# Weight-block sums moved to VectorE and cut into three steps, PSUM pairs evacuated whole, convolution and gelu emitted later in a decoder layer on one Trainium2 core

## The chip, the cores and the metric

The kernel runs on one core of one Trainium2 chip. The metric is device time in microseconds: the median of three runs of the unchanged kernel, beside one execution that the hardware profiler recorded. PE is TensorE, DVE is VectorE, ACT is ScalarE, POOL is GpSimd, and SPq is the queue on SyncE that issues nearly all DMAs.

## What is computed

One inference step of a decoder layer, for 1024 prompt tokens and 8 x 4 sample tokens (T = 1056 columns), model width 1024, feed-forward width 4096, all in fp32:

```
h = rmsnorm(x);  q,k,v,gates = h @ w_in
mix = (sigmoid(gate_a)*(attention_a @ w_branch_a) + sigmoid(gate_b)*(attention_b @ w_branch_b)) @ w_out
x = x + rmsnorm(mix)
a, g = split(rmsnorm(x) @ w_up)              # 1024 -> 4096 and 4096
c = conv_b + sum_j conv_w[j] * shifted(a)    # causal depthwise, width 3
x = x + rmsnorm((gelu(c) * g) @ w_down)      # 4096 -> 1024
```

The change lies in the last stage of the mixer (`@ w_out` and its norm) and in the feed-forward part.

## The kernel before

**fp32 as three products.** Each operand is cut into a high part (fp32r, a cast on ACT) and a low part (operand minus high part). A product is three matmuls, high x high, low x high and high x low, summed in PSUM.

**Strassen over blocks.** `@ w_up` is done as 2 x 2 block products with seven products in place of eight (`PRODUCTS`, L1266). The weights' output side is walked in 32 steps `m`: `m = 2 fp` is the a half (convolution side) of feature block pair `fp`, `m = 2 fp + 1` the g half. In each, product `p` runs 0 to 6 over the blocks A11, A12, S2, S3, A22, S1, S4 of the raw weights, where S1 = A21 + A22, S2 = S1 - A11, S3 = A11 - A21, S4 = A12 - S2. One product is 24 matmuls of 128 x 128 by 264 columns: two column halves `c`, each with its own PSUM bank, four k blocks, three matmuls each. This document calls the seven products of the a half and the seven of the g half of one `fp` a pair of steps: 14 products.

**Order of the products.** `QUEUE` (L1268) is written out by hand: for the first six `m` (`EARLY`) first the products 0 and 1 of each (12 products, while the last norm of the mixer is still being made), then products 2 to 6 of each (30 products), and then seven for each further `m` (182). The engines' instruction streams are in the order of emission; each engine works through its own stream in order.

**What is done ahead.** At the start of product `i`, `up_cut` (L1291) prepares product `i + 4`: the block sums S1, S2, S3, S4 on POOL (L1301 to L1306), then in `cut_block` the cast to the high part on ACT (L1276) and the low part on POOL (L1277). Six `whl` tiles hold the two parts. Raw weights come by DMA into four `raw` tiles, asked for seven products ahead.

**What is done behind.** `evac` (L1351) takes each bank of 264 columns as soon as its 12 matmuls are done: product 0 by an ACT copy (L1357), the others by a DVE addition to a running sum. On the a side the sums land in `at` and `fr` (L1375). After products 5 and 6 of the a side `conv` (L1315) emits the convolution and the gelu of a feature block at once: two ACT instructions (L1320, L1321), four on DVE (L1323, L1324), the gelu on ACT (L1325), two copies on POOL. On the g side DVE multiplies the finished sums into `cv` (L1384). After the last product `u_sums` makes four differences on DVE (L1429 to L1432), which a `store` on SPq sends to DRAM at product 3 of the next step.

**Around it.** The `@ w_out` stage (loop at L1654) runs four column quarters of 264; its norms are made by `post` (L1162), whose steps are hung on the `hook()` calls between the products that follow. For the last quarter these products are the first of `QUEUE`. `spread` (L139) makes a norm: sums of squares by matmuls into a bank `ss`, the root on ACT and DVE, and a matmul into a bank `rb` that spreads the factor. `@ w_down` follows (loop at L1732): seven products of 16 units, `down` (L1547), with 24 matmuls per unit; `down_sum` (DVE), `down_high` (ACT) and `down_low` (weights' low part on POOL L1522, activations' low part on DVE L1523) run 4, 3 and 2 units ahead. `last_weights` (L1525) prepares the weights of the seventh product during the fifth and sixth, cast on ACT and low part on POOL. All PSUM tiles come from one pool of eight banks, `bank()`.

Of the kernel before, what the change touches and what calls it, by code (L numbers as in the profile page):

```python
# [48 lines left out]
def trunk(ctx, tc, a):  # L49
# [10 lines left out]
    psum = ctx.enter_context(tc.tile_pool(name="psum", bufs=8, space=PSUM))  # L60
# [78 lines left out]
    def spread(sums, w=CH, new=None):  # L139
# [3 lines left out]
        ss = bank("ss")  # L143
# [9 lines left out]
        rb = bank("rb")[:, 0:w]  # L153
# [950 lines left out]
    c_stack.close()  # L1104
    xpool = ctx.enter_context(tc.tile_pool(name="xpool", bufs=1, side="right", reuse_waits="tile"))
# [56 lines left out]
    def post(q, sums):  # L1162
# [108 lines left out]
    LA = 4  # L1271
# [8 lines left out]
    uraw, usum, uhl = {}, {}, {}  # L1280
# [34 lines left out]
    def conv(f):  # L1315
        at, fr, cv = fs[f]
# [20 lines left out]
    def put_a(f, q, emit):  # L1337

        at, fr = fs[f][0:2]
        n = CQ if q < NQ - 1 else CQ - NS  # L1340
        emit(at[:, 2 + q * CQ:2 + q * CQ + n], slice(0, n))
        if n < CQ:
            emit(fr[:, :, 2:6], slice(n, CQ))

    def seen(cols, t):
        t = t[:, cols]
        return t.rearrange("p (b s) -> p b s", s=4) if cols.stop - cols.start == NS else t

    scratch = []

    def evac(m, p, c, ps):  # L1351
        fp, part = divmod(m, 2)
        f = 2 * fp
        cs = slice(c * CQ, (c + 1) * CQ)
        s, t = u1[m], u2.get(m)
        if p == 0:
            act.copy(s[:, cs], ps)  # L1357
            return
        if p == 2:
            dve.tensor_tensor(s[:, cs], ps, s[:, cs], op=OP.add)  # L1360
            if m in ug1:
                cv = fs[f][2]
                dve.tensor_tensor(cv[:, cs], ug1[m][:, cs], cv[:, cs], op=OP.mult)
            return
        if p == 3:
            dve.tensor_tensor(t[:, cs], ps, s[:, cs], op=OP.add)
            return
        if p == 5:
            dve.tensor_tensor(s[:, cs], ps, s[:, cs], op=OP.add)

        fo = f + (p in (4, 5))
        base = t if p in (4, 5) else s
        q = c + 2 * (p in (5, 6))
        if part == 0:
# [531 lines left out]
```

## Time and profile before

| | us |
|---|---|
| median of 3 runs | 1925.26 |
| lowest and highest | 1924.42, 1927.51 |
| profiled execution, device time | 1927.82 |
| profiled execution, span of the core | 1925.8 |
| PE busy in the span | 1851.3 (96%) |
| DVE, ACT, POOL busy | 1206.2 (63%), 728.3 (38%), 1009.5 (52%) |
| mean granted TensorE clock, share of full speed | 0.986 |

The time of a run is the span plus about two microseconds around it. Matmuls are pipelined: a row gives a start, a time until the last modelled end, a count, and in square brackets the idle time before it with the instruction that ended it. Rows of one stream overlap by the depth of the pipeline, so the pace of PE is read from one start to the next.

### The profile page before, as it was taken

The numbers are of one execution on the slowest core, as the hardware profiler recorded it, in microseconds if no ns is written. First come the engines' busy times: TensorE is split into PE (matmuls) and PEld (weight loads), VectorE is DVE, ScalarE is ACT, GpSimd is POOL, SyncE is SP. The second block draws the span as 40 slices with busy tenths as digits, with TensorE's granted clock in tenths as the row PEclk, the third lists the DMA queues.
The fourth block names the chain that finished last, engine by engine and source line by source line (L and its number), as shares of the span: only waits on it lengthen the run. The fifth ranks groups of instructions, "written<-read, shape, count | busy, mean of one in ns | idle before, by whom it ended". The sixth has DMA issues, their size and how long they took to land.

```text
span 1925.8 us, 35025 instructions
## 1 busy us (share of the span) xinstructions
PE 1851.3 (96%) x13714; PEld 1764.4 (92%) x13714; DVE 1206.2 (63%) x2367; ACT 728.3 (38%) x1673; POOL 1009.5 (52%) x819
## 2 busy tenths in 40 slices
PE   8999999999999999989889999999999999999897
PEld 7977788888999999988879999999999999999897
DVE  8354427877720114659677666667776668778885
ACT  4366554434221115443323333333233334443541
POOL 3200015434422321355777888778878856555863
PEclk9999999999999999998999999999999999999998
DMA  7111225434622225762332332222323256635343
GB/s 250 55 62 68 80 70 178 146 111 130 201 94 95 80 98 176 268 217 74 137 122 95 112 100 85 84 84 95 106 90 111 79 184 223 208 123 187 112 134 130
DMA packets 102100, 243.35 MB, mean 126 GB/s; under 512 B 20416, under 2 KB 40960, under 8 KB 99200
## 3 DMA queue, kind: packets, MB, share of 16 engines
q1 hardware_dynamic: 100272, 240.63, 37.3%
q8 instruction: 108, 1.77, 0.4%
q10 hardware_dynamic: 1664, 0.49, 0.1%
q14 instruction: 56, 0.46, 0.1%
HBM read 197.83 MB, written 88.11 MB: 148 GB/s over the span
## 4 chain that ended last, share of the span: by engine, by line
PE 66%; POOL 16%; DVE 7%; issue 7%; ACT 3%; DMA 1%; SPq 0%; POOLq 0%; DVEq 0%; ACTq 0%
PE dense L232 32%; PE dense L1566 13%; PE dense L1410 12%; POOL whl L1277 8%; PE S L414 2%; PE O L486 2%; PE PT L474 2%; ACT whl L1276 2%; POOL raw L1306 1%; POOL S L1302 1%; POOL S L1301 1%; POOL raw L1304 1%; POOL ncv L1326 1%; DVE cv L1323 1%; DVE uc L1523 1%
## 5 line engine op out<-in xcount | busy, mean ns | idle before, releaser
L1410 PE MATMUL dense<-T,whl 128*128 128x264 f32 x3072 | 395.7, 288 | 28.0 <-POOL whl L1277 14.6
L1410 PEld LDWEIGHTS dense<-T,whl 128*128 128x128 f32 x3072 | 383.9, 191 | 36.9 <-POOL whl L1277 19.7
L232 PE MATMUL dense<-hh,wh 128*128 128x352 f32 x960 | 322.9, 339 | 0.7 <-ACT wh L97 0.2
L232 PE MATMUL dense<-hl,wh 128*128 128x352 f32 x960 | 310.6, 327 | 2.3 <-DVE hl L189 2.2
L232 PE MATMUL dense<-hh,wl 128*128 128x352 f32 x960 | 308.1, 324 | 0.6 <-DVE wl L98 0.6
L98 POOL TENSOR_TENSOR wl<-raw,wh 128x1024 fp32r<-128x1024 f32 (+1 forms) x46 | 106.4, 2314 | 378.0 <-ACT wh L97 375.7
L1410 PE MATMUL dense<-B,whl 128*128 128x264 f32 x2304 | 289.4, 285 | 9.5 <-ACT whl L1276 6.7
L1566 PE MATMUL dense<-uc,whl 128*128 128x264 f32 x2328 | 289.1, 286 | 8.0 <-DVE uc L1523 5.8
L1566 PEld LDWEIGHTS dense<-uc,whl 128*128 128x128 f32 x2328 | 286.3, 189 | 10.1 <-DVE uc L1523 7.1
L1410 PEld LDWEIGHTS dense<-B,whl 128*128 128x128 f32 x2304 | 284.7, 190 | 10.8 <-ACT whl L1276 7.3
L1277 POOL TENSOR_TENSOR whl<-raw,whl 128x512 fp32r<-128x512 f32 x160 | 221.1, 1400 | 121.7 <-ACT whl L1276 121.6
L232 PEld LDWEIGHTS dense<-hh,wh 128*128 128x128 f32 x960 | 181.6, 190 | 21.3 <-issue 14.0
L232 PEld LDWEIGHTS dense<-hl,wh 128*128 128x128 f32 x960 | 180.8, 189 | 3.2 <-DVE hl L189 3.2
L232 PEld LDWEIGHTS dense<-hh,wl 128*128 128x128 f32 x960 | 181.4, 190 | 1.2 <-DVE wl L98 1.2
L1276 ACT CAST whl<-raw 128x512 fp32r<-128x512 f32 x160 | 91.4, 615 | 171.4 <-POOL raw L1306 111.0
L1522 POOL TENSOR_TENSOR whl<-wr,whl 128x512 fp32r<-128x512 f32 x64 | 100.5, 1586 | 72.9 <-ACT whl L1509 72.9
L1323 DVE SCALAR_TENSOR_TENSOR cv<-a,cw,cv 128x1024 f32<-128x1024 f32 x64 | 82.1, 1282 | 89.8 <-ACT cv L1320 89.8
L1523 DVE TENSOR_TENSOR uc<-ur,uc 128x528 fp32r<-128x528 f32 x96 | 115.7, 1218 | 8.8 <-ACT uc L1507 8.7
L1277 POOL TENSOR_TENSOR whl<-S,whl 128x512 fp32r<-128x512 f32 x64 | 88.9, 1389 | 37.9 <-ACT whl L1276 37.9
L1276 ACT CAST whl<-S 128x512 fp32r<-128x512 f32 x64 | 39.9, 624 | 175.8 <-POOL S L1302 175.8
L1384 DVE TENSOR_TENSOR cv<-scratch,cv 128x264 f32<-128x264 f32 x116 | 100.1, 863 | 4.0
L1125 POOL TENSOR_TENSOR sq<-sq 128x264 f32<-128x264 f32 x39 | 34.8, 893 | 112.7 <-ACT sq L1665 91.0
(309 smaller groups left out, 3188.6 us busy)
## 6 DMA issues: line engine op xcount, KB each, us to landing
raw<-in_w_up SPq DMA_DIRECT2D x70, 512.0 KB
out_s<-in_cache SPq DMA_DIRECT2D x32, 1022.0 KB
ur<-ud SPq DMA_DIRECT2D x112, 264.0 KB
raw<-in_w_in SPq DMA_DIRECT2D x40, 512.0 KB
ud<-ts SPq DMA_DIRECT2D x16, 1056.0 KB
kv<-in_kv_s SPq DMA_DIRECT2D x64, 256.0 KB
wr<-in_w_down SPq DMA_DIRECT2D x48, 256.0 KB
ud<-cv SPq DMA_DIRECT2D x16, 528.0 KB
```

The costliest lines, as they stand in the source:

```text
L98: (eng or pool).tensor_tensor(l, raw, as32(h), op=OP.subtract)
L232: pe.matmul(ps, lhsT=w, rhs=x, start=(i == 0), stop=(i == len(mm) - 1))
L414: pe.matmul(S[h][:, 0:nk], lhsT=q[r, i * 128:(i + 1) * 128], rhs=k[r, blocks[i][0] * 128:blocks[i][0] * 128 + nk], start=True, stop=True)
L474: pe.transpose(PT[:, o:o + 128], s["P"][:, h, j * 128:(j + 1) * 128], ident)
L1276: act.copy(t[:, 0], src)
L1277: pool.tensor_tensor(t[:, 1], src, as32(t[:, 0]), op=OP.subtract)
L1323: dve.scalar_tensor_tensor(o, at[:, x:x + SEQ], w[x], o, op0=OP.mult, op1=OP.add)
L1384: dve.tensor_tensor(cv[:, qs], o, cv[:, qs], op=OP.mult)
L1410: pe.matmul(ps, lhsT=l, rhs=r, start=(k == 0 and n == 0), stop=(k == 3 and n == 2))
L1522: pool.tensor_tensor(dw[i][:, 1], dsrc.pop(i), as32(dw[i][:, 0]), op=OP.subtract)
L1523: dve.tensor_tensor(dx[i][:, 1], x[:, fp % 2], as32(dx[i][:, 0]), op=OP.subtract)
L1566: pe.matmul(dbanks[j, c], lhsT=l, rhs=r, start=(x == 0 and n == 0), stop=(x == FP - 1 and n == 2))
```

## The change

- **Three steps in place of one.** `up_cut` and `cut_block` are split. At the start of product `i`, `up_low(i + 3)` emits the low part on POOL, then `up_sum(i + 5)` the block sums, now on DVE, then `up_high(i + 4)` the cast on ACT. Before all of these stood at `i + 4`, with the sums on POOL.
- **PSUM in pairs of banks.** From the `@ w_out` stage on, PSUM is a ring of four tiles of two banks (`bank2`). The two column halves of a product share one tile, and one instruction of 528 columns evacuates both after the second half. `spread` takes `ss` and `rb` from the two banks of one tile. `down` and `down_evac` do likewise.
- **Convolution later.** `conv` becomes `conv_1` (all but the gelu) and `conv_2` (the gelu). For the block finished by product 5, `conv_1` comes after product 6; its gelu, and the other block's `conv_1`, one product later; the other gelu one more. The four differences of `u_sums` are handed out one per column half over the next two products (`spare`).
- **Smaller moves.** In the last quarter of `@ w_out` the residual additions of `post` are all on DVE, one addition of squares fewer is on POOL, raw weights of the first products are asked for from the first `ct` on, and no cache copy is issued there. In `@ w_down` the weights of the seventh product are all prepared in the sixth, low part on DVE; the sums of the fourth product's result (`down_sums`) are 12 instructions of 528 columns in place of 24 of 264, and one of them per unit in place of two.

```diff
@@
+    def bank2(name):
+        return pairs_of_banks[0].tile([128, 2, 512], F32, name=name, tag="pair", bufs=4)
...
-        ss = bank("ss")
+        if pairs_of_banks:
+            two = bank2("ss")
+            ss, rb = two[:, 0], two[:, 1]
...
-            (dve if ct % 2 else pool).tensor_tensor(m, m, x3[q][ct // 4][:, ct % 4], op=OP.add)
+            (dve if ct % 2 or last else pool).tensor_tensor(m, m, x3[q][ct // 4][:, ct % 4], op=OP.add)
...
-                if ct in (1, 2, 3, 5):
+                if ct in (1, 3, 5):
...
-    def cut_block(src):
-
-        t = wpool.tile([128, 2, 512], F32R, name="whl", tag="W", bufs=6)
-        act.copy(t[:, 0], src)
-        pool.tensor_tensor(t[:, 1], src, as32(t[:, 0]), op=OP.subtract)
-        return t
...
-            pool.tensor_tensor(s1, a21, a22, op=OP.add)
-            pool.tensor_tensor(s2, s1, a11, op=OP.subtract)
+            dve.tensor_tensor(s1, a21, a22, op=OP.add)
+            dve.tensor_tensor(s2, s1, a11, op=OP.subtract)
         elif p == 3:
-            pool.tensor_tensor(a21, a11, a21, op=OP.subtract)
+            dve.tensor_tensor(a21, a11, a21, op=OP.subtract)
         elif p == 6:
-            pool.tensor_tensor(a12, a12, usum[m][1], op=OP.subtract)
+            dve.tensor_tensor(a12, a12, usum[m][1], op=OP.subtract)
...
+    def up_high(i):
+        if i < len(QUEUE):
+            uhl[i] = wpool.tile([128, 2, 512], F32R, name="whl", tag="W", bufs=6)
+            act.copy(uhl[i][:, 0], usrc[i])
+
+    def up_low(i):
+        if i < len(QUEUE):
+            pool.tensor_tensor(uhl[i][:, 1], usrc.pop(i), as32(uhl[i][:, 0]), op=OP.subtract)
+
+    def up_ahead(i):
+
+        up_loads(i + 7)
+        up_low(i + 3)
+        up_sum(i + 5)
+        up_high(i + 4)
...
+        ps = bank2("dense")
         for c in range(2):
-            ps = bank("dense")[:, 0:CQ]
...
-            evac(m, p, c, ps)
+            if c:
+                evac(m, p, ps)
             hook()
-        if part == 0 and p in (5, 6):
-            fo = f + (p == 5)
-            fs[fo].append(T_("cv"))
-            conv(fo)
+            if spare:
+                spare.popleft()()
+        if after:
+            after.popleft()()
+        if part == 0 and p == 6:
+            conv_1(f + 1)
+            after.append(lambda: (conv_2(f + 1), conv_1(f)))
+            after.append(lambda: conv_2(f))
...
-        pool.tensor_tensor(wk[fp][:, 1], x, as32(wk[fp][:, 0]), op=OP.subtract)
+        dve.tensor_tensor(wk[fp][:, 1], x, as32(wk[fp][:, 0]), op=OP.subtract)
...
-        if p == 4 and fp >= 4:
-            last_weights(fp - 4)
-        elif p == 5 and fp < 4:
-            last_weights(FP - 4 + fp)
+        if p == 5:
+            last_weights(fp)
...
-            if q == NQ - 1 and ct > 3:
-                up_loads(2 * (ct - 4))
+            if q == NQ - 1:
+                up_loads(min(2 * ct, 6))
...
-        if i + LA < len(QUEUE):
-            up_cut(*QUEUE[i + LA])
+        up_ahead(i)
...
-        advance(2)
+        advance(1 if p == 4 else 2)
```

POOL, in the steady part of the products (seven per step): `whl` is a weight tile with both parts, `S` and `raw` are the block sums. Before:

```order
L1277 TENSOR_TENSOR whl<-S,whl 128x512
L1306 TENSOR_TENSOR raw<-raw,S 128x512
L1277 TENSOR_TENSOR whl<-raw,whl 128x512 x3
L1301 TENSOR_TENSOR S<-raw 128x512
L1302 TENSOR_TENSOR S<-S,raw 128x512
L1277 TENSOR_TENSOR whl<-S,whl 128x512
L1304 TENSOR_TENSOR raw<-raw 128x512
```

Now:

```order
L1324 TENSOR_TENSOR whl<-S,whl 128x512
L1324 TENSOR_TENSOR whl<-raw,whl 128x512 x3
L1324 TENSOR_TENSOR whl<-S,whl 128x512
L1324 TENSOR_TENSOR whl<-raw,whl 128x512
L1362 MEMSET a 128x2
```

Four sums of each step have left POOL; the seven low parts stay.

ACT, from the last products of an a side into the g side (`cv<-a` is the start of a convolution, `cv<-cv` a gelu, `scratch<-dense` the evacuation of product 0 of the g side). Before:

```order
L1276 CAST whl<-S 128x512
L1320 ACTIVATE cv<-a,cw 128x1024
L1321 ACTIVATE cv<-fr,cw 128x32
L1325 ACTIVATE cv<-cv 128x1056
L1276 CAST whl<-raw 128x512
L1320 ACTIVATE cv<-a,cw 128x1024
L1321 ACTIVATE cv<-fr,cw 128x32
L1325 ACTIVATE cv<-cv 128x1056
L1276 CAST whl<-raw 128x512
L1357 COPY scratch<-dense 128x264 x2
L1276 CAST whl<-S 128x512
```

Now:

```order
L1320 CAST whl<-S 128x512
L1320 CAST whl<-raw 128x512
L1346 ACTIVATE cv<-a,cw 128x1024
L1347 ACTIVATE cv<-fr,cw 128x32
L1320 CAST whl<-raw 128x512
L1380 COPY scratch<-dense 128x528
L1356 ACTIVATE cv<-cv 128x1056
L1346 ACTIVATE cv<-a,cw 128x1024
L1347 ACTIVATE cv<-fr,cw 128x32
L1320 CAST whl<-S 128x512
L1356 ACTIVATE cv<-cv 128x1056
```

A cast and the evacuation now stand between the first convolution and its gelu, and one cast between the second and its gelu.

DVE, in the same place, from the second convolution to product 3 of the g side. Before:

```order
L1323 SCALAR_TENSOR_TENSOR cv<-a,cw,cv 128x1024
L1324 SCALAR_TENSOR_TENSOR cv<-fr,cw,cv 128x32
L1381 TENSOR_TENSOR scratch<-dense,scratch 128x264
L1384 TENSOR_TENSOR cv<-scratch,cv 128x264
L1381 TENSOR_TENSOR scratch<-dense,scratch 128x264
L1384 TENSOR_TENSOR cv<-scratch,cv 128x264
L1360 TENSOR_TENSOR scratch<-dense,scratch 128x264 x2
L1366 TENSOR_TENSOR scratch<-dense,scratch 128x264 x2
```

Now:

```order
L1349 SCALAR_TENSOR_TENSOR cv<-a,cw,cv 128x1024
L1350 SCALAR_TENSOR_TENSOR cv<-fr,cw,cv 128x32
L1313 TENSOR_TENSOR raw<-raw,S 128x512
L1399 TENSOR_TENSOR scratch<-dense,scratch 128x528
L1383 TENSOR_TENSOR scratch<-dense,scratch 128x528
L1402 TENSOR_TENSOR cv<-scratch,cv 128x528
L1383 TENSOR_TENSOR scratch<-dense,scratch 128x528
L1308 TENSOR_TENSOR S<-raw 128x512
L1309 TENSOR_TENSOR S<-S,raw 128x512
```

The block sums (`raw<-raw,S`, `S<-raw`, `S<-S,raw`) stand among the evacuations, and each two evacuations of 264 columns are one of 528.

## Rows read from the trace of the kernel before

**Rows 1.** Windows: us, busy (count) PE, PEld, DVE, ACT, POOL; clock, DMA, GB/s.

```profile
841.57:868.47 26.90, 20.50 (x158) 20.12 (x157) 13.01 (x29) 9.33 (x24) 16.51 (x20) 0.91 0.56 200
868.47:909.46 40.99, 37.49 (x271) 36.95 (x272) 40.20 (x64) 17.82 (x35) 20.54 (x15) 0.89 0.18 60
909.46:1008.40 98.94, 81.70 (x627) 77.23 (x626) 69.44 (x120) 31.96 (x46) 75.03 (x66) 1.00 0.37 127
1008.40:1566.57 558.17, 541.39 (x4370) 536.26 (x4369) 383.16 (x657) 185.64 (x321) 446.73 (x391) 0.99 0.29 97
```

**Rows 2.** Windows of one pair of steps, early and steady; columns as in rows 1.

```profile
912.38:949.96 37.58, 30.79 (x238) 29.09 (x237) 27.60 (x46) 12.13 (x17) 28.86 (x25) 1.00 0.40 140
...
1129.54:1172.30 42.76, 41.31 (x337) 40.90 (x337) 29.01 (x51) 13.95 (x24) 34.19 (x31) 1.00 0.30 95
```

**Rows 3.** Timeline of PE, steady part: start, us, count, idle before.

```profile
1092.62 8.89 PE L1410 MATMUL dense<-B,whl 128*128 128x264 f32 x72
1101.35 11.82 PE L1410 MATMUL dense<-T,whl 128*128 128x264 f32 x96
...
1128.46 0.39 PE L1410 MATMUL dense<-T,whl 128*128 128x264 f32 x1 [0.74 <-ACT scratch L1357]
1129.54 5.98 PE L1410 MATMUL dense<-T,whl 128*128 128x264 f32 x47 [0.70 <-POOL whl L1277]
...
1171.22 0.39 PE L1410 MATMUL dense<-T,whl 128*128 128x264 f32 x1 [0.76 <-ACT scratch L1357]
```

**Rows 4.** Timeline of ACT and POOL where the a side ends.

```profile
1083.78 1.09 ACT L1325 ACTIVATE cv<-cv 128x1056 f32<-128x1056 f32 x1 [2.57 <-DVE cv L1324]
...
1085.45 1.29 POOL L1277 TENSOR_TENSOR whl<-raw,whl 128x512 fp32r<-128x512 f32 x1 [3.00 <-ACT whl L1276]
```

**Rows 5.** Timeline of PE in the early products 2 to 6, one period apart.

```profile
928.96 0.39 PE L1410 MATMUL dense<-B,whl 128*128 128x264 f32 x1 [2.22 <-ACT whl L1276]
...
966.55 0.39 PE L1410 MATMUL dense<-B,whl 128*128 128x264 f32 x1 [2.21 <-ACT whl L1276]
```

**Rows 6.** Timeline of DVE and POOL: instructions with and without the other engine beside.

```profile
1083.50 0.24 DVE L1324 SCALAR_TENSOR_TENSOR cv<-fr,cw,cv 128x32 f32<-128x32 f32 x1
1102.07 0.71 DVE L1432 TENSOR_TENSOR ts<-cv,ts 128x528 f32<-128x528 f32 x1
1118.41 1.28 DVE L1323 SCALAR_TENSOR_TENSOR cv<-a,cw,cv 128x1024 f32<-128x1024 f32 x1
1118.52 2.32 POOL L1304 TENSOR_TENSOR raw<-raw 128x512 f32<-128x512 f32 x1
1119.61 1.27 DVE L1324 SCALAR_TENSOR_TENSOR cv<-fr,cw,cv 128x32 f32<-128x32 f32 x1
1761.38 0.68 DVE L1491 TENSOR_TENSOR wr<-wr 128x512 f32<-128x512 f32 x1
```

**Rows 7.** Lines by form, 1086 to 1560 us: count, busy, mean ns, idle before.

```profile
L1384 DVE TENSOR_TENSOR cv<-scratch,cv 128x264 f32<-128x264 f32 x90 | 78.4, 871 | 3.1
L1381 DVE TENSOR_TENSOR scratch<-dense,scratch 128x264 f32<-128x264 f32 x90 | 37.9, 421 | 24.5 <-ACT scratch L1357 23.2 <-PE dense L1410 1.3
L1323 DVE SCALAR_TENSOR_TENSOR cv<-a,cw,cv 128x1024 f32<-128x1024 f32 x44 | 56.4, 1282 | 53.5 <-ACT cv L1320 53.5
L1430 DVE TENSOR_TENSOR ts<-cv 128x528 f32<-128x528 f32 x11 | 19.8, 1798 | 0.0
```

**Rows 8.** Timeline of ACT and PE at the last norm of the mixer.

```profile
847.74 0.62 ACT L1276 CAST whl<-raw 128x512 fp32r<-128x512 f32 x1 [2.50 <-DMA raw<-in_w_up]
851.50 0.83 PE L156 MATMUL rb<-dg,ones 128*128 128x128 f32 x6 [2.61 <-DVE dg L151]
865.47 3.15 PE L147 MATMUL ss<-ones,sq 128*128 128x1 f32 x14 [2.77 <-DVE sq L1181]
```

**Rows 9.** Timeline of PE, fifth product of `@ w_down`, first and last wait of five.

```profile
1781.20 3.20 PE L1566 MATMUL dense<-uc,whl 128*128 128x264 f32 x24 [0.32 <-DVE uc L1523]
...
1801.82 25.02 PE L1566 MATMUL dense<-uc,whl 128*128 128x264 f32 x191 [1.98 <-DVE uc L1523]
```

More of the change, by code (lines that the diff above doesn't have):

```diff
@@ L142, in spread @@
         np_ = -(-w // 128)
-        ss = bank("ss")
+        if pairs_of_banks:
+            two = bank2("ss")
+            ss, rb = two[:, 0], two[:, 1]
+        else:
+            ss, rb = bank("ss"), None
         for s in range(np_):
@@ L152, in spread @@
         yield
-        rb = bank("rb")[:, 0:w]
+        rb = (bank("rb") if rb is None else rb)[:, 0:w]
         for s in range(np_):
@@ L1335, in new_a, with two @@
         fs[f] = [at, fr]
[L1337 to L1347, printed above, removed]
     scratch = []
-    def evac(m, p, c, ps):
+    def two(t):
+        return t.rearrange("p (c t) -> p c t", c=2)
@@ L1352, in evac @@
+    def evac(m, p, ps):
         fp, part = divmod(m, 2)
         f = 2 * fp
-        cs = slice(c * CQ, (c + 1) * CQ)
         s, t = u1[m], u2.get(m)
+        h1, h2 = slice(0, 2 * CQ), slice(2 * CQ, T)
+        both = ps[:, :, 0:CQ]
         if p == 0:
-            act.copy(s[:, cs], ps)
+            act.copy(two(s), both)
             return
[L1359 to L1363, printed above, removed]
-            return
@@ L1365, in evac @@
[L1365 to L1374, printed above, removed]
-            put_a(fo, q, lambda o, z: dve.tensor_tensor(o, seen(z, ps), seen(z, base[:, cs]), op=OP.add))
-            return
-        if p == 1 and m in ug1:
-            dve.tensor_tensor(ug1[m][:, cs], ps, s[:, cs], op=OP.add)
-            return
@@ L1380, in evac @@
-        o = scratch[0][:, 6 * CQ + c * CQ:7 * CQ + c * CQ] if p in (1, 4) else base[:, cs]
-        dve.tensor_tensor(o, ps, base[:, cs], op=OP.add)
-        cv = fs[fo][2]
-        qs = quarter_of(q)
-        dve.tensor_tensor(cv[:, qs], o, cv[:, qs], op=OP.mult)
-    def up(m, p):
+        if p in (2, 3, 5):
+            dve.tensor_tensor(two(t if p == 3 else s), both, two(s), op=OP.add)
+        if part == 0:
+            at, fr = fs[f + (p in (4, 5))][0:2] if p != 3 and p != 2 else (None, None)
+            base = t if p in (4, 5) else s
+            if p in (1, 4):
+                dve.tensor_tensor(two(at[:, 2:2 + 2 * CQ]), both, two(base), op=OP.add)
+            elif p in (5, 6):
+                n = CQ - NS
+                dve.tensor_tensor(at[:, 2 + 2 * CQ:2 + 3 * CQ], ps[:, 0, 0:CQ], base[:, 0:CQ], op=OP.add)
+                dve.tensor_tensor(at[:, 2 + 3 * CQ:2 + SEQ], ps[:, 1, 0:n], base[:, CQ:CQ + n], op=OP.add)
+                dve.tensor_tensor(fr[:, :, 2:6], *(x.rearrange("p (b s) -> p b s", s=4) for x in (ps[:, 1, n:CQ], base[:, CQ + n:2 * CQ])),
+                                  op=OP.add)
+            return
@@ new lines, in evac @@
+        tm = scratch[0][:, 6 * CQ:8 * CQ] if scratch else None
+        c11 = ug1.get(m, tm)
+        if p == 1:
+            dve.tensor_tensor(two(c11), both, two(s), op=OP.add)
+        if p == (4 if m in ug1 else 2):
+            cv = fs[f][2][:, h1]
+            dve.tensor_tensor(cv, c11, cv, op=OP.mult)
+        if p == 4:
+            cv = fs[f + 1][2][:, h1]
+            dve.tensor_tensor(two(tm), both, two(t), op=OP.add)
+            dve.tensor_tensor(cv, tm, cv, op=OP.mult)
+        elif p in (5, 6):
+            o, cv = (t, fs[f + 1][2][:, h2]) if p == 5 else (s, fs[f][2][:, h2])
+            dve.tensor_tensor(two(o), both, two(o), op=OP.add)
+            dve.tensor_tensor(cv, o, cv, op=OP.mult)
@@ L1556, in down @@
             if x == 0:
-                dbanks[j, c] = bank("dense")[:, 0:CQ]
+                if p < NP and c == 0 or p == NP and j % 2 == 0 or p > NP:
+                    dbank = bank2("dense")
+                dbanks[j, c] = dbank[:, c if p < NP else j % 2 if p == NP else 0, 0:CQ]
+                if p < NP:
+                    dpairs[j] = dbank
             ks = slice(128 * j, 128 * j + 128)
@@ L1569, in ac, with ac2, down_evac @@
         return acc[k // 2][:, k % 2, quarter_of(q)]
-    def down_evac(p, js):
+    def ac2(k, half):
+        return acc[k // 2][:, k % 2, 2 * CQ * half:2 * CQ * half + 2 * CQ]
+    def down_evac(p):
         tm = {}
-        for j, c in js:
-            ps = dbanks[j, c]
-            c11, c12, c21 = ac(j, c), ac(j, 2 + c), ac(4 + j, c)
+        for j in range(4):
+            ps = dpairs[j][:, :, 0:CQ]
+            c11, c12, c21 = ac2(j, 0), ac2(j, 1), ac2(4 + j, 0)
             if p in (0, 1, 2):
-                o = (c11, c21, c12)[p]
-                if (j + c) % 2:
+                o = two((c11, c21, c12)[p])
+                if j % 2:
                     act.copy(o, ps)
@@ L1681, in trunk @@
                 sp.dma_start(stc, a["state"])
[L1682 removed]
+            if ct % 2 and q < NQ - 1:
                 copy_rows()
@@ L1708, in trunk @@
             copy_rows()
+    while spare:
+        spare.popleft()()
     while stores:
@@ L1714, in trunk @@
     step = iter(())
-    ALL = [(j, c) for j in range(4) for c in range(2)]
     def advance(n):
```

93 lines of the change are left out of this document (58 added, 35 removed).

## The prediction

> **What bounds the kernel now.** I read the windows by stage first. PE is busy all but a few per cent nearly everywhere, so the question is only how far its pace lies under its best. That pace comes from two starts in the steady part: 72 matmuls of 264 columns between 1092.62 and 1101.35 [rows 3], 8.73 us, or 0.1213 us each; a product of 24 takes 2.91 us. Held against the windows [rows 1] this gives the loss of each stage. From 841.57 the five products 0 to 4 need 14.6 us and the norms' small matmuls some 3.5; the window has 26.9, so 8.8 are lost. The next 11 products need 32.0 and 0.7 of norm in 41.0: 8.3 lost. The 26 products to 1008.40 need 75.7 in 98.9: 23.2 lost. The 182 after them need 529.6 in 558.2: 28.6 lost. Before 841 hardly anything is lost that the change touches, and in `@ w_down` some 10 us.
>
> What ends the waits differs by stage. In the steady part one pair of steps takes 42.76 us from one wait to its like (1128.46 to 1171.22 [rows 3]), against 14 x 2.91 = 40.7. The whole excess of 2.0 sits in one place, 0.74 behind ACT and 0.70 behind POOL, plus two drained pipelines: a cast and then its low part come too late. The cause stands earlier in ACT's stream [rows 4]: the gelu had waited 2.57 us for DVE's convolution, the cast stands behind it, and POOL, with nothing else to do, waited 3.00 us for that cast. In the early products the pair's period is 37.6 (928.96 to 966.55 [rows 5]) against 10 x 2.91 = 29.1, with 2.2 us at a single wait.
>
> **DVE and POOL hold each other up.** A copy of 32 columns takes 0.24 us when POOL is quiet and 1.27 right behind a POOL sum; that sum took 2.32, having begun beside a 1.28 us DVE instruction, where 1.29 [rows 4] is the time of its size alone [rows 6]. An addition of 264 columns from SBUF has a mean of 0.87, while one that reads PSUM keeps 0.42 through 90 instances [rows 7]. So DVE instructions with both tensors in SBUF and POOL's take turns, and PSUM evacuations do not. I add what takes turns in a pair of steps, each at its time alone. Before, DVE: eight multiplications at about 0.43, four differences at 0.71 and four times 1.28 + 0.24 for the convolutions, 12.4 us. POOL: 22 instructions of 1.29 and about 1 us of small copies, 29.4; in the early pairs, which have 10 products, 18 of them, 24.2. Sums: 41.8 steady and 36.6 early, against periods of 42.76 and 37.6. Both are within 3% of the period: what takes turns is as full as PE, and in the early pairs it is the bound.
>
> **The block sums move.** Eight sums a pair leave POOL (8 x 1.29 = 10.3 us) and come to DVE at 0.68 alone [rows 6]: 5.4. The eight multiplications become four of 528 columns at about 0.71. What takes turns is then 12.4 + 5.4 - 0.6 = 17.2 for DVE (0.6 from the merged multiplications) plus 14 or 10 low parts and the copies, 19.1 (steady) or 13.9 (early), for POOL: 36.3 and 31.1, with the 3% 37.4 and 32.0. Steady, that is 3.3 us under PE's 40.7. Early it is 2.9 over 29.1. DVE alone: 29.0 busy in a steady pair [rows 2], plus 8 sums at between 0.68 and 1.80 (the contended mean [rows 7]), less about 3 for merged instructions (ten evacuations of 2 x 0.42 become about 0.69 each, an estimate from 264 more columns at the slope of 0.43 to 0.71). At 1.0 per sum, nearer the low end because POOL's busy share falls from 80% to about half, DVE has 34 of 40.7. Early it is 27.6 + 8.0 - 2.5 = 33 of 29.1, so there both sums say that a pair takes 32 to 33, not 29.1.
>
> By the Trainium skill (SBUF — State Buffer, "SBUF: two separate sides") DVE with two SBUF inputs and GpSimd share a port pair by an exclusive lock, held for a whole instruction. The rows agree (0.24 against 1.27). Without such a lock the early pairs would run at PE's 29.1; with it they come out as above.
>
> **Casts and low parts a product apart; convolution and gelu later.** In the steady part the cast that came late now has, in ACT's stream, a cast and an evacuation ahead of a gelu whose convolution was emitted a product earlier. DVE needs about 3 us for that convolution, a product lasts 2.91, so the gelu waits a microsecond at most, and the cast behind it still has three products until its matmuls. The sum is a product ahead of the cast: DVE may be some 6 us late before PE notices. I follow DVE through the end of an a side: it is at most 5 us behind, in the g side's product 1, and caught up by product 3. So the 2.0 us should go, 13 times, which is 26 of the 28.6. I count 25 (18 if a third of the wait stays, 28 if nothing does). Early: 26 products are 2.6 pairs that lose 2.9 to 4 us each where 23.2 are lost now, a gain of 13 to 16; I take 15 (8 to 21).
>
> **The pairs of banks.** Evacuation begins half a product later and the ring holds four products, so PE meets it only when DVE is three products (8.7 us) late. One place is tighter: `spread` now holds a tile from `ss` to the last reader of `rb`, and the fourth product after it needs that tile. In the second norm (about 860 us) that reader stands behind some 5 us of differences on DVE. I price it at up to 3.6 us, inside the next term.
>
> **The last norm of the mixer.** The 2.61 us wait of `rb` came from ACT's root standing behind a cast that waited for raw weights from DRAM; these are now asked for four column tiles earlier, with no cache copy ahead of them, so it goes. The 2.77 and its 1 us neighbour came from additions that went DVE, POOL, ACT, POOL; with all residual additions on DVE eight tiles cost 8 x (0.42 + about 0.5), some 7.5 us, where rb to the sums took 14 [rows 8]. I count 7.5 of the 8.8 (4 to 9). In the next window DVE is full (40.20 of 40.99 [rows 1]) and gets seven sums more, 4.8 us, against fewer POOL collisions and merged evacuations: -1 (-6 to +3).
>
> **`@ w_down`.** Five waits in the fifth product, 0.32 to 1.98, 5.2 us in all [rows 9], come from DVE taking turns with two POOL low parts a unit. One of the two leaves for the sixth product, onto DVE, and DVE has one 528 addition per unit in place of two of 264. The unit is then 0.68 + 0.71 + 0.71 + 1.29 = 3.4 in turns, against 2.91, for 12 units: still some 2 us late. The sixth product gets the same crowding with its squares. Net 4 (-3 to +8). The way into `@ w_down`: 1 (-1 to 2).
>
> **The sum.** 7.5 - 1 + 15 + 25 + 1 + 4 = 51.5. The profiled execution took 1927.8 with a span of 1925.8; it would become 1876 and 1874. The median of the runs is 2.6 below the profiled one: 1925.3 - 51.5 = 1874.
>
> **Rivals.** (1) DVE takes POOL's place wherever products come thick. For it: its 98% in the window from 868 and the early 33 of 29.1. If the early 42 products gain nothing, there remain 25 + 1 + 4 = 30: 1895. Against it: what takes turns falls by 5.7 a pair. (2) The change goes slower: each moved sum costs DVE the contended 1.80, and its idle waits stay. A steady pair is 29.0 + 14.4 - 3 and the 4.9 us per pair that DVE waits for ACT's first convolution step (53.5 over 11 pairs [rows 7]), 45.3 against 42.76: 13 x 2.5 = 33 lost, and early (27.6 + 14.4 - 2.5 + 4 = 43.5) 2.6 x 5.9 = 15 more; 1925 + 48 = 1973. It decides from 1.5 us per sum on. Against it: POOL's share falls at the same time. (3) All waits go, the early ones too: 8.8 + 3 + 21 + 28 + 2 + 8 = 71 would be the ceiling, and two thirds of what the forecast leaves gives 1861. (4) The cast is late still, for a reason in ACT's stream that I don't see, and only small gains are left, within 0.2%.
>
> **How the numbers follow.** Forecast, 1862 to 1888: 0.62. Rival 1, 1888 to 1900: 0.17. Rival 3, under 1862: 0.12. Rival 4: 0.04. Rival 2: 0.05. The range must leave out no more than 0.2: 1859 to 1897 leaves out rivals 2 and 4, the upper end of 1 and half of 3. Faster by over 0.2% (3.9 us, about what a measurement of this kernel can tell from no change): 0.91; within: 0.04; slower: 0.05.
>
> **What would show it.** Steady pairs at 40.7 to 41.2 us from start to start with no PE wait on the low part; POOL busy about 22 of them, DVE 32 to 36. Early pairs at 31 to 34, with the remaining waits behind DVE or behind ACT casts that wait for DVE sums. The small matmuls of the second norm at 860 in place of 868. In `@ w_down` fewer waits in the fifth product and some in the sixth. Steady pairs over 42 with DVE busy above 38 would make the prediction wrong, and so would waits of PE on a bank whose evacuation is queued on DVE.

## The result and the profile after

| | before | after |
|---|---|---|
| median, us | 1926.35 | 1880.22 |
| lowest and highest of four runs | 1924.42, 1927.51 | 1878.56, 1881.13 |
| ratio to before, 95% interval | | 0.9761, 0.9744 to 0.9777 |
| span of the profiled execution | 1925.8 | 1876.7 |
| first up matmul | 841.6 | 857.7 |
| up stage, to the first matmul of `@ w_down` | 725.0 | 669.3 |
| from there to the end | 359.2 | 349.7 |

The forecast was 1874 (1859 to 1897). The time lies 6.2 us above the forecast, but it is made otherwise than the sum said: the up stage and `@ w_down` gained 65.2 us where 51.5 were expected, and 16.1 were lost in the stage ahead of them, where the prediction expected no change. The profiled execution is the fastest of the four, so stages add up to 49.1 us where the medians differ by 46.1. The windows of after, columns as in [rows 1], the same four stages (from the first matmuls of products 0, 5, 16 and 42) and then an early and a steady pair as in [rows 2]:

```profile
857.69:876.86 19.17, 19.17 (x164) 19.17 (x163) 13.85 (x30) 9.53 (x21) 12.04 (x15) 1.00 0.42 132
876.86:918.10 41.24, 35.26 (x273) 34.51 (x272) 40.45 (x64) 18.45 (x33) 14.39 (x12) 0.96 0.21 65
918.10:995.79 77.69, 76.17 (x627) 75.81 (x625) 74.88 (x101) 30.23 (x44) 47.12 (x44) 1.00 0.43 159
995.79:1527.02 531.23, 530.73 (x4368) 530.54 (x4369) 463.39 (x552) 189.67 (x297) 316.03 (x290) 1.00 0.32 109
932.67:961.80 29.13, 29.13 (x242) 29.13 (x241) 28.61 (x40) 10.66 (x16) 17.02 (x16) 1.00 0.47 172
1014.13:1054.93 40.80, 40.80 (x339) 40.80 (x338) 36.71 (x46) 15.41 (x24) 25.30 (x23) 1.00 0.42 148
```

PE is busy in all of the first window and in nearly all of the third and fourth. The early pair runs at PE's own 29.1 us, though DVE is busy in 28.6 of it; the next takes 30.2, with one wait. At PE's pace of 2.91 us a product, products 16 to 41 still lose 2.0 us, and those behind them 1.6. Only products 5 to 15 lose as much as before the change, with DVE full.

The new loss lies ahead of all this, where `mixed @ w_out` runs. The windows of that stage, before and after:

```profile
738.00:841.60 103.60, 103.60 (x861) 103.60 (x860) 62.34 (x154) 47.23 (x117) 31.18 (x38) 1.00 0.67 227
```

```profile
736.20:857.70 121.50, 107.56 (x860) 104.54 (x859) 62.68 (x155) 47.54 (x117) 30.33 (x38) 1.00 0.55 182
```

The same matmuls take 121.5 us instead of 103.6, at full clock in both. What PE waits for there, by the view of waits (us in total, times, longest):

```profile
PE dense L242 <- ACT mixed L1715: 13.9, 16, 1.4
```

Sixteen waits for 32 column tiles (four quarters, eight each). Now PE and ACT around two of them in the timeline:

```profile
838.49 0.28 PE L242 MATMUL dense<-ml,woh 128*128 128x264 f32 x1
840.07 0.39 PE L242 MATMUL dense<-mh,woh 128*128 128x264 f32 x1 [1.30 <-ACT mixed L1715]
...
847.03 0.39 PE L242 MATMUL dense<-mh,wh 128*128 128x264 f32 x1 [0.85 <-ACT mixed L1715]
```

```profile
846.22 0.39 ACT L1714 ACTIVATE sq<-dense 128x264 f32<-128x264 f32 x1 [1.75 <-PE dense L242]
846.50 0.48 ACT L1715 ACTIVATE mixed<-dense,gains 128x264 f32<-128x264 f32 x1
```

The even column tile's product ends, ACT reads its bank twice until 846.98, and only then the odd one's first matmul goes, at 847.03. It writes the other bank, but of the same two-bank tile: the changed loop takes `pair_ = bank2("dense")` for two column tiles, and the program orders accesses by tile, so the write of one half waits for the readers of the other. Against 0.12 us from start to start, 838.49 to 840.07 costs 1.5.

### The profile page after: what moved, and what is told of

Its sections match the earlier page's. It is cut to its first block, busy times and chain, and to the rows that moved or that the text cites. A ratio compares the mean times of both kernels' runs of the same rounds, so it can differ in the third digit from the quotient of the medians.

```text
span 1876.7 us, 34608 instructions
## 1 busy us (share of the span) xinstructions
PE 1828.5 (97%) x13720; PEld 1750.5 (93%) x13720; DVE 1291.5 (69%) x2229; ACT 731.4 (39%) x1635; POOL 813.0 (43%) x670
## 4 chain that ended last, share of the span: by engine, by line
PE 45%; DVE 5%; issue 1%; ACT 1%; POOL 0%; DVEq 0%; ACTq 0%; POOLq 0%
PE dense L1437 27%; PE dense L1603 17%; DVE cv L1349 1%; DVE cv L1350 1%; DVE scratch L1383 0%; DVE raw L1313 0%; DVE S L1308 0%; ACT cv L1346 0%; DVE a L1383 0%; DVE uc L1554 0%; DVE cv L1410 0%; PE ss L157 0%; ACT cv L1356 0%; PE ss L166 0%; DVE acc L1693 0%
## 5 line engine op out<-in xcount | busy, mean ns | idle before, releaser
L1437 PE MATMUL dense<-T,whl 128*128 128x264 f32 x3072 | 380.8, 285 | 5.6 <-DVE a L1388 3.6
L1437 PEld LDWEIGHTS dense<-T,whl 128*128 128x128 f32 x3072 | 377.1, 189 | 6.3 <-ACT whl L1320 3.8
L1324 POOL TENSOR_TENSOR whl<-raw,whl 128x512 fp32r<-128x512 f32 x160 | 244.4, 1540 | 125.2 <-ACT whl L1320 121.2
L1324 POOL TENSOR_TENSOR whl<-S,whl 128x512 fp32r<-128x512 f32 x64 | 99.3, 1552 | 110.5 <-ACT whl L1320 110.5
L1554 DVE TENSOR_TENSOR uc<-ur,uc 128x528 fp32r<-128x528 f32 x96 | 107.9, 1132 | 9.5 <-ACT uc L1538 9.5
L1349 DVE SCALAR_TENSOR_TENSOR cv<-a,cw,cv 128x1024 f32<-128x1024 f32 x64 | 83.6, 1306 | 32.7 <-ACT cv L1346 32.7
L1540 ACT CAST whl<-wr 128x512 fp32r<-128x512 f32 x64 | 39.8, 622 | 76.8 <-POOL whl L1553 25.3
```

What stands on the lines that cost most here:

```text
L1324: pool.tensor_tensor(uhl[i][:, 1], usrc.pop(i), as32(uhl[i][:, 0]), op=OP.subtract)
L1349: dve.scalar_tensor_tensor(o, at[:, x:x + SEQ], w[x], o, op0=OP.mult, op1=OP.add)
L1437: pe.matmul(ps[:, c, 0:CQ], lhsT=l, rhs=r, start=(k == 0 and n == 0), stop=(k == 3 and n == 2))
L1540: act.copy(dw[i][:, 0], dsrc[i])
L1554: dve.tensor_tensor(dx[i][:, 1], x[:, fp % 2], as32(dx[i][:, 0]), op=OP.subtract)
```

## Experiments

All times are medians in us. The stages are read from the first matmuls of each profiled execution; the first up matmul of kernels that share the tile as after does varies from 856.9 to 860.5. The columns "16 to 41" and "42 on" are the times of these products, two parts of the up stage.

| kernel | first up matmul | 16 to 41 | 42 on | up stage | rest | time | ratio to before |
|---|---|---|---|---|---|---|---|
| before | 841.6 | 98.9 | 558.2 | 725.0 | 359.2 | 1926.4 | |
| after | 857.7 | 77.7 | 531.2 | 669.3 | 349.7 | 1880.2 | 0.9761 (0.9744 to 0.9777) |
| e1 own tile in `w_out` | 839.0 | 77.7 | 530.9 | 669.0 | 350.9 | 1863.5 | 0.9675 (0.9659 to 0.9691) |
| e2 sums on POOL | 859.7 | 79.7 | 530.4 | 673.2 | 349.4 | 1884.3 | 0.9777 (0.9763 to 0.9792) |
| e3 conv at once | 857.4 | 84.3 | 530.4 | 675.1 | 348.7 | 1883.3 | 0.9775 (0.9760 to 0.9790) |
| e4 no lead | 860.5 | 82.8 | 531.6 | 676.4 | 349.4 | 1886.5 | 0.9790 (0.9775 to 0.9804) |
| e5 low part as before, `w_down` | 859.2 | 77.6 | 531.2 | 669.3 | 357.1 | 1888.0 | 0.9795 (0.9781 to 0.9810) |
| e6 none of e2, e3, e4's three | 856.9 | 99.4 | 563.9 | 725.7 | 350.0 | 1937.6 | 1.0052 (1.0037 to 1.0067) |
| e7 before, with sums and lead | 840.9 | 84.4 | 531.1 | 681.1 | 358.0 | 1881.0 | 0.9758 (0.9742 to 0.9775) |
| e8 evacuations of one bank | 859.5 | 78.9 | 532.5 | 672.0 | 349.8 | 1881.6 | 0.9764 (0.9750 to 0.9779) |
| e9 e6 with the lead | 860.3 | 88.2 | 532.3 | 683.7 | 349.6 | 1895.6 | 0.9834 (0.9819 to 0.9848) |
| e10 e6 with sums on DVE | 859.3 | 85.9 | 530.4 | 678.3 | 348.6 | 1889.1 | 0.9801 (0.9786 to 0.9815) |
| e11 e6 with conv put off | 857.5 | 87.5 | 564.9 | 714.8 | 352.3 | 1927.6 | 1.0006 (0.9996 to 1.0015) |
| e12 e1, low parts to POOL | 841.4 | 77.0 | 530.9 | 673.5 | 349.5 | 1866.7 | 0.9684 (0.9669 to 0.9698) |

### The loss in the stage of w_out (e1)

```diff
-            if ct % 2 == 0:
-                pair_ = bank2("dense")
-            ps = pair_[:, ct % 2, 0:CQ]
+            ps = bank2("dense")[:, 0, 0:CQ]
```

> The changed kernel, but in the stage of `w_out` each column tile `ct` has a two-bank tile of its own, of which it uses one bank. Theory: the loss of 16.1 us ahead of the first up product (841.57 before, 857.69 after) comes from odd column tiles that share a tile with the even one, so that their first matmul waits for ScalarE to have read the even one's bank (16 waits, 13.9 us in the trace of after). Then these waits are gone, the first up product starts at 842 to 845, and the time is 1864 to 1868 us. Rival: the loss comes from the ring of PSUM tiles being four long instead of eight, one of them held by the norm: then a tile for each column tile makes it worse, the waits on ScalarE stay in another place, and the time is 1880 or more.

1863.5 us. The view of waits shows none of PE in this stage any more, and its window is

```profile
736.00:839.00 103.00, 103.00 (x857) 103.00 (x856) 61.76 (x154) 46.91 (x117) 31.14 (x38) 1.00 0.65 215
```

The theory holds: half of each tile is thrown away, the ring is still four long, and 16.8 us come back, a little more than the theory's range. This version beats both kernels.

### One part of the up stage undone (e2, e3, e4)

e2 puts the four lines of block sums back on POOL:

```diff
-            dve.tensor_tensor(s1, a21, a22, op=OP.add)
+            pool.tensor_tensor(s1, a21, a22, op=OP.add)
...
```

> The changed kernel, but the sums of the up weight blocks are back on GpSimd; they still run a product ahead of the casts. Theory A: in the 182 steady products it was the lead that took the waits away, since GpSimd has room there (34.2 us busy of a pair's 42.8 before), while in the early products GpSimd's own work (28.9 us for a pair of 29.1 us of matmuls) sets the pace: no or few waits after product 41, about 2 to 4 us a pair lost before it, 1885 to 1892 us. Theory B: it was GpSimd's load that made the weights late, so that the losses of products 16 to 41 and of the steady ones (23.2 and 28.6 us before) mostly return: 1915 to 1932 us.

e3 issues convolution and gelu at once:

```diff
-        if part == 0 and p == 6:
-            conv_1(f + 1)
-            after.append(lambda: (conv_2(f + 1), conv_1(f)))
-            after.append(lambda: conv_2(f))
+        if part == 0 and p in (5, 6):
+            conv_1(f + (p == 5))
+            conv_2(f + (p == 5))
```

> The changed kernel, but convolution and gelu of a block are issued right after the evacuation that completes it, as before the change (product 5 for the one block, 6 for the other). Theory: in the changed order VectorE is already the busiest engine (28.6 us of a pair's 29.1 in the early products), and a gelu that waits for its convolution on ScalarE holds up the cast behind it; the weights have more than two products of lead, so only the early products notice: 1880 to 1886 us. Rival: putting it off is what keeps the casts on time in every pair, and without it each of the 13 steady pairs loses 1 to 2 us: 1893 to 1906 us.

e4 issues sum, cast and low part together:

```diff
         up_loads(i + 7)
-        up_low(i + 3)
-        up_sum(i + 5)
-        up_high(i + 4)
+        up_sum(i + 4)
+        up_high(i + 4)
+        up_low(i + 4)
```

> The changed kernel, but sum, cast and low part of a block are issued together four products ahead of their use, as before the change; the sums stay on VectorE. Theory: a cast waits on ScalarE for a sum that stands behind VectorE's late evacuations, and everything behind it comes later, the low part last; 11.6 us of lead are eaten up where VectorE is three products late, so the early products lose 10 to 15 us and the steady ones under 5: 1888 to 1900 us. Rival A: the sums' engine was all that mattered: 1879 to 1883 us. Rival B: the lead was all that mattered: losses as before the change, 1920 us or more.

1884.3, 1883.3 and 1886.5: each costs 3 to 6 us of the 46 that the change gains, all of it before product 42, and the heavy rivals (1893 and more) fall; e2 and e4 come out 1 to 2 us under the ranges of their theories. e2 bears on the prediction's picture of turns as well. It has POOL's old load, and its early pair reads

```profile
934.60:963.70 29.10, 29.02 (x239) 28.81 (x238) 26.36 (x32) 10.08 (x15) 29.02 (x23) 1.00 0.49 174
```

POOL is busy in all but 0.1 of it, DVE in 26.4, and PE hardly waits. Its pairs take 29.5 and 32.7 us (products that read B, 922.88 to 952.39 and 952.39 to 985.09); the prediction counted 36.6 for this mix, 36.0 with the merged multiplications. In the second, POOL is busy for 32.5 us, and PE waits for it:

```profile
968.97 4.44 PE L1437 MATMUL dense<-B,whl 128*128 128x264 f32 x23 [1.72 <-POOL whl L1324]
```

### The three undone together, and one at a time put back (e6, e9, e10, e11)

e6 is after with the three edits above; merged evacuations, the norm, the loads and `@ w_down` stay as changed.

> The changed kernel with three things undone together: the sums of weight blocks are on GpSimd, sum, cast and low part are issued together four products ahead, and convolution and gelu come at once. What stays of the change in the up stage is that two banks are evacuated by one instruction (and the norm and the loads ahead of it). Singly, the three cost 4.1, 6.3 and 3.1 us. Theory: each covers for the others, and without all three the casts and low parts are late again in most pairs, 14 us or more lost beyond the sum of the three: 1908 to 1922 us. Rival: they add up and no more, since the merged evacuations are what made room on VectorE: 1890 to 1897 us.

1937.6 us, beyond even the theory's range, and slower than before, since e6 keeps the loss in `w_out`. Its up stage takes 725.7, as long as before, though the norm's gain is in it; products 42 on take 5.8 longer than before. The steady part, PE, then ACT and POOL in the timeline:

```profile
1138.11 0.39 PE L1437 MATMUL dense<-T,whl 128*128 128x264 f32 x1 [1.67 <-ACT scratch L1380]
1138.96 6.01 PE L1437 MATMUL dense<-T,whl 128*128 128x264 f32 x47 [0.47 <-POOL whl L1324]
```

```profile
1135.97 1.08 ACT L1356 ACTIVATE cv<-cv 128x1056 f32<-128x1056 f32 x1 [2.57 <-DVE cv L1350]
1136.96 0.60 ACT L1320 CAST whl<-raw 128x512 fp32r<-128x512 f32 x1
1137.47 0.59 ACT L1380 COPY scratch<-dense 128x528 f32<-128x528 f32 x1
```

```profile
1137.64 1.27 POOL L1324 TENSOR_TENSOR whl<-raw,whl 128x512 fp32r<-128x512 f32 x1 [3.00 <-ACT whl L1320]
```

This is the chain of [rows 4], to the same 2.57 and 3.00 us: the gelu waits for its convolution, cast and evacuation stand behind it, POOL idles for the cast. With merged evacuations PE's first wait has even grown, from 0.74 [rows 3] to 1.67. ACT's copy behind the gelu now frees two banks and takes 0.59 us; that is the smaller part of the growth, and no run shows where the rest comes from.

e9 is e6 with the lead back (`up_low(i + 3)`, `up_sum(i + 5)`, `up_high(i + 4)`, as in after):

> The kernel of e6 with one of the three things put back: the sums (on GpSimd) a product ahead of the casts, and the low parts a product behind them. Convolution and gelu still come at once. In e6 a steady pair is held up where the gelu waits 2.6 us on ScalarE for its convolution, the cast behind it comes late, GpSimd idles 3.0 us for that cast and then cannot catch up. Theory A: any one of the three breaks that chain, since without any one of them the changed kernel loses only 3 to 6 us: 1884 to 1893 us. Theory B: a lead alone only shifts the chain by a product; GpSimd still has sums, low parts and its idle wait to fit into a pair: 1905 us or more.

e10 is e6 with `dve.tensor_tensor` in the four sums:

> The kernel of e6 with one of the three things put back: the sums of weight blocks are on VectorE. Sum, cast and low part are issued together, convolution and gelu at once. Theory A: with 10 us of sums a pair gone GpSimd catches up after each late cast, so nearly all of the loss goes: 1886 to 1895 us. Theory B: the late cast itself (ScalarE behind its gelu) holds the matmuls, whoever adds the blocks, and VectorE's sums now stand behind the convolution too: 1905 us or more.

e11 is e6 with the four lines of `conv_1` and `conv_2` of after:

> The kernel of e6 with one of the three things put back: the second convolution and both gelus are put off by a product. Sums are on GpSimd, and sum, cast and low part are issued together. Theory A: the gelu's wait of 2.6 us is the root of the late casts, so that in the steady pairs the waits go and only the early pairs, where GpSimd is full (28.9 of 29.1 us), lose some 15 us: 1893 to 1903 us. Theory B: the gelu's wait is only one of several: casts also wait for GpSimd's sums (3.3 us in e6 at one place), and most of the loss stays: 1915 us or more.

e9 takes 1895.6, between its theories and nearer A; e10 1889.1, theory A; e11 1927.6, theory B. With after, e2, e3, e4 and e6 these are all eight combinations of the three. One window of the steady part, from e6, e9, e10 and e11 in this order:

```profile
1100.00:1500.00 400.00, 384.12 (x3093) 379.79 (x3093) 244.48 (x315) 125.12 (x199) 320.86 (x276) 0.99 0.30 97
```

```profile
1100.00:1500.00 400.00, 400.00 (x3293) 399.93 (x3292) 255.49 (x334) 136.72 (x216) 315.33 (x295) 1.00 0.30 100
```

```profile
1100.00:1500.00 400.00, 400.00 (x3297) 400.00 (x3296) 299.25 (x413) 136.80 (x216) 222.99 (x216) 1.00 0.31 102
```

```profile
1100.00:1500.00 400.00, 384.95 (x3107) 383.33 (x3106) 263.77 (x313) 127.59 (x206) 311.14 (x279) 0.98 0.30 96
```

The lead by itself, or DVE sums by themselves, take every wait out of the steady part. Put-off convolution by itself gains nothing there (its 10 us under e6 come from products 16 to 41): DVE has the second convolution ahead of the g side's evacuation, and PE waits for that instead. DVE and PE of e11:

```profile
1128.59 1.29 DVE L1349 SCALAR_TENSOR_TENSOR cv<-a,cw,cv 128x1024 f32<-128x1024 f32 x1 [2.29 <-ACT cv L1346]
...
1130.99 2.35 DVE L1349 SCALAR_TENSOR_TENSOR cv<-a,cw,cv 128x1024 f32<-128x1024 f32 x1
...
1133.43 0.69 DVE L1399 TENSOR_TENSOR scratch<-dense,scratch 128x528 f32<-128x528 f32 x1
```

```profile
1134.27 4.69 PE L1437 MATMUL dense<-T,whl 128*128 128x264 f32 x24 [2.18 <-DVE scratch L1399]
```

The early products need more than one of the three. In e9 PE waits for a cast and its low part in every pair (940.46, then 974.86: 34.4 us a pair where after has 29.1 and 30.2), and ACT's cast stands behind a gelu that has waited 4.62 us. A wait can cost more than its length: behind these two the granted clock has a mean of 0.62 from 942.01 to 946.45, so that part of it is at the lower of the two levels, and the 23 matmuls take 4.4 us, where at 0.1213 each they would take 2.8.

```profile
940.46 0.39 PE L1437 MATMUL dense<-B,whl 128*128 128x264 f32 x1 [2.28 <-ACT whl L1320]
942.01 4.60 PE L1437 MATMUL dense<-B,whl 128*128 128x264 f32 x23 [1.16 <-POOL whl L1324]
...
974.86 0.39 PE L1437 MATMUL dense<-B,whl 128*128 128x264 f32 x1 [2.01 <-ACT whl L1320]
```

```profile
938.82 1.08 ACT L1356 ACTIVATE cv<-cv 128x1056 f32<-128x1056 f32 x1 [4.62 <-DVE cv L1350]
939.81 0.60 ACT L1320 CAST whl<-raw 128x512 fp32r<-128x512 f32 x1
```

### Without pairs of banks (e7, e8)

e7 is the kernel before with `up_sum`, `up_high`, `up_low` and `up_ahead` of after in place of `up_cut`, and the earlier loads; every tile is one bank.

> The kernel before, with the sums of weight blocks on VectorE and a product ahead of casts and low parts, and the loads of the first weights four column tiles earlier; evacuation bank by bank, convolution, gelu, norm and `@ w_down` as before the change, so no bank shares a tile. Theory: without merged evacuations VectorE has 29.0 + 8 x 1.2 = 38.6 us of a steady pair's 40.7, still room, but 27.6 + 8 x 1.0 = 35.6 of an early pair's 29.1, so the steady products gain some 20 us and the early ones nothing: 1902 to 1912 us. Rival A: lead and sums by themselves do what the change does in the whole up stage: 1878 to 1890 us. Rival B: VectorE's evacuations come late in every pair: 1920 us or more.

e8 splits each merged instruction of the up stage:

```diff
+    def halves(o, x, y, op):
+        for c in range(2):
+            dve.tensor_tensor(o[:, c], x[:, c], y[:, c], op=op)
...
-            dve.tensor_tensor(two(c11), both, two(s), op=OP.add)
+            halves(two(c11), both, two(s), OP.add)
```

> The changed kernel, but in the up stage each evacuation, addition and multiplication of two banks is issued as two instructions of one bank each, one behind the other, at the same place; nothing else differs, the tiles stay of two banks. Theory: this costs VectorE about 0.15 us for each extra instruction, some 2 us a pair; in the steady pairs there is room (36.7 of 40.8 us), in the early ones, where VectorE is busy 28.6 of 29.1 us, 1.5 to 2 us a pair come on top, and products 5 to 15 lose about 2 us: 1885 to 1890 us. Rival: VectorE's lateness is covered by the three products that the ring of tiles allows: 1879 to 1882 us.

e7 takes 1881.0, as much as the whole change: 43.9 of its 55.7 us in the up stage, and nothing lost in `w_out`. What it lacks is 4.6 in the first five products (23.8 us against 19.2), where the norm is as before; 6.7 in products 16 to 41, which take as long as in e3, where convolution and gelu also come at once; and 8.3 in `@ w_down`. My expectation for it (early products gain nothing) was wrong, its rival A right. e8 adds 2.7 to the up stage and 1.4 to the time, less than the runs can tell, as its rival said: merged evacuations are worth next to nothing here. That their halves share a tile should cost nothing in the up stage, since both are read after both are written; no run tests it by itself.

### The low part in w_down (e5)

```diff
-        dve.tensor_tensor(wk[fp][:, 1], x, as32(wk[fp][:, 0]), op=OP.subtract)
+        pool.tensor_tensor(wk[fp][:, 1], x, as32(wk[fp][:, 0]), op=OP.subtract)
...
-        if p == 5:
-            last_weights(fp)
+        if p == 4 and fp >= 4:
+            last_weights(fp - 4)
+        elif p == 5 and fp < 4:
+            last_weights(FP - 4 + fp)
...
-        advance(1 if p == 4 else 2)
+        advance(2)
```

> The changed kernel, but in `@ w_down` the low parts of the last product's weights are back on GpSimd and at their old place (four of eight in the fifth product, four in the sixth), and the stream of sums and squares is advanced by two in every unit, as before the change. Theory: of the 9.5 us that `@ w_down` gained, most came from taking that low part out of the fifth product, where it stood with two others on GpSimd: the five waits of 0.32 to 1.98 us return in part, 1884 to 1889 us. Rival: the gain came from evacuating and summing two banks at once, and the place of the low part hardly matters: 1879 to 1883 us.

1888.0, as the theory had it. Of the 9.5 us, 7.4 go again, and the waits of [rows 9] are back in the form below. The run puts back two things at once, the low part and the pace of two additions a unit, now of 528 columns each; how much each of them costs it doesn't show.

```profile
PE dense L1605 <- POOL whl L1553: 2.7, 4, 1.1
PE dense L1605 <- DVE uc L1554: 2.5, 3, 1.4
```

### What is left: products 5 to 15 (e12)

```diff
-            op_cut(name, j, src, c)
+            op_cut(name, j, src, c, pool if j and name != "T2" else dve)
```

> The kernel of e1 (a tile for each column tile in the stage of `w_out`), and of the low parts of the second operands, which VectorE makes during products 1 to 13 of the up stage, those of `j` = 1 of T3, T4, B22 and T1 (8 of 20) go to GpSimd, which is idle 27 of the 42 us there. Theory: the waits left there (3.6 us for an evacuation that stands behind eight low parts on VectorE, and 0.9) come from VectorE's load; 8 x 0.75 = 6 us leave it, most of these waits go: 1858 to 1861 us. Rival: GpSimd's work there stretches VectorE's by as much as it takes off it, or delays the weights' low parts: 1863 us or more.

1866.7: the rival, 3.2 above e1, with the up stage 4.5 longer, all of it in products 5 to 15. The longest wait there is, in e1,

```profile
PE dense L1437 <- DVE a L1388: 3.6, 1, 3.6
```

and in e12 it has changed its owner and grown to 4.24 us; POOL and DVE of that stretch:

```profile
889.29 5.36 PE L1437 MATMUL dense<-T,whl 128*128 128x264 f32 x24 [4.24 <-POOL whl L1324]
```

```profile
897.07 1.80 POOL L1163 TENSOR_TENSOR T<-mixed,T 128x528 fp32r<-128x528 f32 x1
898.82 1.72 POOL L1324 TENSOR_TENSOR whl<-raw,whl 128x512 fp32r<-128x512 f32 x1
```

```profile
897.60 1.82 DVE L1313 TENSOR_TENSOR raw<-raw,S 128x512 f32<-128x512 f32 x1
899.34 1.77 DVE L1163 TENSOR_TENSOR T<-mixed,T 128x528 fp32r<-128x528 f32 x1
```

The weights' low parts stand on POOL behind the operands', and while both engines work, DVE's instructions of 0.69 take 1.8. POOL's idle time there was no room for them.

## Why the prediction was right in the time and wrong in its terms

**The stage of `w_out`: the step that failed.** "Before 841 hardly anything is lost that the change touches" answers the wrong question: nothing was lost there to be gained, but the edit to the loop over `ct` was in the diff, and it had a cost. The paragraph on pairs of banks asked only how late evacuation may come in a ring of four. It did not ask what lies between the writes of a tile's two halves. In the up stage nothing does; in `w_out` ACT reads the first half in between. 16 waits, 16.1 us at the first up matmul, and e1 shows them to be this.

**The last norm, 7.5.** 26.9 us became 19.2, a gain of 7.7, with no wait left in it and the granted clock up from 0.91 to 1.00. Right, in both its parts: in e7, whose norm is as before, the earlier loads bring 3.1 of it, and the wait for the squares, 3.1 there, is left. The window behind it: -1 forecast, -0.25 measured, and e12 shows that DVE's load there can't simply be handed to POOL.

**Early products, 15 (8 to 21).** The window went from 98.9 to 77.7 us, a gain of 21.2: rival 3 is nearly what happened. The failed step is the bound of 32 to 33 us for an early pair, which took 29.1 and 30.2; both sums behind it were too high.

The first was the count of turns. I added up the times alone of all instructions that hold each other up (31.1, with 3% 32). Where both engines work without a gap (e12, above), one subtraction on DVE and one on POOL together take 1.74 us, from 897.60 to 899.34, not 0.69 + 1.29 = 1.98. The Trainium skill (SBUF — State Buffer, "SBUF: two separate sides") has the lock held for a whole instruction; the rows agree that each stretches the other, but the sum of the times alone is too high by a seventh. Scaled by 1.74/1.98, an estimate, 31.1 is 27.3, under PE's 29.1, and the 36.0 of e2's mix is 31.6, near the mean of its two pairs, 31.1. (The two instructions that the prediction calls a copy and an addition in its evidence are a step of the convolution and a multiplication; their times are as it says.)

The second was DVE's load: 33 us were counted, 28.6 measured. In that pair the eight sums took 6.6 instead of 8.0, and the other instructions 22.0 instead of 25.1.

So the old period of 37.6 was not set by turns, as I had read it: e2 runs the same mix, but for the merging, in 31.1, and e9, with the same turns as e2 but the gelu at once, takes 34.4 through waits for late casts.

**Steady products, 25.** 558.2 to 531.2, 27.0, and pairs of 40.8. The size is right, its reason only half. I credited the put-off convolution first and the lead second. By e9 and e10 the lead or the moved sums each suffice alone, and by e11 the put-off convolution alone does not; what it contributes lies in the early products, 3.1 us of the time beside both others (e3), but 11.3 beside the lead alone (e9 against e2). How much of the gain belongs to lead and how much to sums has no answer: together they overlap almost wholly.

**Merged evacuations, about 2.5 us of DVE a pair.** The instruction is as cheap as estimated (0.70 for 528 columns), but DVE had the time: 1.4 us of 1880 (e8). I had let it help pay for the early pairs.

**`@ w_down`, 4 (-3 to +8), and 1 for the way in.** 9.5 measured. All five waits of the fifth product went and none came in the sixth; e5 puts 7.4 of it on taking the third low part out of the fifth product together with the slower pace of the sums. The mechanism was named; the units that I expected to stay 2 us late did not, 3.4 us of turns by my count against 2.91, which 1.74/1.98 brings to 3.0 by the same estimate.

**The rivals.** Rival 1 (DVE takes POOL's place early) and rival 2 (contended sums make it slower) fell, and rival 4 with them: behind product 42 no wait of PE is on a cast. For rival 2, in the steady part three of the four kinds of sum take a mean of 1.16 to 1.65 us, so the price was near; the 36.7 us that DVE then needs (32 to 36 were expected) still fit in 40.8. Rival 3's 1861 is nearly e1's 1863.5: without the shared tile nearly all waits but those of products 5 to 15 go, as it said.

The balance: 9.2 more in the up stage and 4.5 more in `@ w_down` than forecast, 16.1 less in `w_out`: 51.5 + 13.7 - 16.1 = 49.1, the difference of the spans. The forecast came close by luck, from errors of opposite sign.

## What to carry to other kernels

Where a tile is widened, look at every loop that takes its parts one by one: if a part is read before the next is written, the widening turns overlap into a wait, and the order of instructions shows it before any run. When several cures are applied at once, undoing each singly says only that the others cover for it; put each back alone as well: here that separated two cures that suffice in the steady part from one that does nothing there. And a busy share of 98% is no loss by itself: it is one only where a wait names that engine.

## What the runs showed of the hardware that was not expected

DVE and POOL subtractions side by side take 1.74 us a pair, 12% less than the 1.98 of their times alone; and PE ran at its pace through 29.1 us of early products in which POOL was busy 29.0 and DVE 26.4 (e2), before it waited 1.72 us for POOL in the next pair.
